# A two-layer decoder trunk on one core: the up projection in seven products of halves as well, in an order that interleaves two pairs

## The chip, the core and the metric

One core of a Trainium2 chip runs the whole program. The metric is the device time of one execution in microseconds (us), as the median over runs; a profile of one further execution gives the trace. TensorE multiplies (a weight load, then a matmul that streams columns), VectorE (DVE) and ScalarE (ACT) do the elementwise work, GpSimd (POOL) a little, and SyncE (SP) issues the DMAs.

## The reference, cut to what matters

The input is 512 tokens of 1024 features in float32. There are two layers; each is a feed-forward block (FFN), a mixer, and another FFN, so four FFNs in all:

```
def swiglu(h, w_gate, w_up, w_down):
    return (jax.nn.silu(h @ w_gate) * (h @ w_up)) @ w_down
...
h = rmsnorm(x, ffn1_norm[i])
x = x + FFN_HALF * swiglu(h, ffn1_w_gate[i], ffn1_w_up[i], ffn1_w_down[i])
```

The inner width is 2816, which is 22 tiles of 128 columns. The mixer of layer 0 pools over windows of tokens; that of layer 1 is latent attention with 8 heads. The change touches only the FFNs, and through one pool of buffers the rest.

## The kernel before

**Layout and precision.** Activations lie with features in partitions: eight tiles of 128 features by 512 tokens. Every float32 operand is cut into a high and a low part (`split`, L114 to L118: ScalarE copies the high part, VectorE subtracts to get the low one), and a product of two operands is three matmuls, high by high, high by low, low by high (`mm3`). So a product of one weight tile (1024 features by 128 columns) with all tokens is 8 x 3 = 24 matmuls of 512 columns. All of them are issued at L106.

**An FFN.** The 22 tiles of gate and up go in thirds: tiles 0 to 7, 8 to 15, 16 to 21. After each third its part of the down projection runs (eight output tiles, L479 adds them to x). Tiles 0 to 3 use x unscaled. From tile 4 on the operand is the normed x (`xn`), and the gate's tiles are taken two at a time by Winograd's form of Strassen's product: `class Two` with seven products of halves in place of eight. A half is 512 features by 256 tokens or by 128 columns of weights, so one such product (`block`) is 4 x 3 = 12 matmuls of 256 columns, and a pair takes 7 x 12 = 84 of them.

**What a pair costs besides.** `w_sums` loads the two weight tiles (L340, L341), makes four sums of their quarters on VectorE (L350, 512 columns each), and splits a11 with a12, s1 with s2, s3 with s4 (1024 columns each) and a22 (512). The products go into two accumulators, each a whole bank, both halves of which are used. Their partial sums are combined by one copy on ScalarE (L379) and five additions of 256 columns on VectorE (L395); silu is L287, the product with up L291.

**Order.** In the thirds from tile 8 on, a pair of tiles is written as: the up product of tile f (`product`, weights by `load_w` with its DMA at L129), the first four blocks of the gate's pair (`begin`), the up product of tile f + 1, the last three blocks (`end`), then silu, multiplication and split. In the first third the four up products of tiles 4 to 7 come first, with the sums of xn (`x_sums`) between them, then the two gate pairs.

**Buffers.** Weights: `raw` 3 buffers, `whi` and `wlo` 3 each; `chi`, `clo` 2 each and `s` 2 for the sums; a22's halves 1 each. `work` has 7, PSUM accumulators 6. The order of instructions on each engine is made by a list scheduler of the framework from the order in the text, and semaphores keep it; each engine then takes its instructions in that order.

Of the kernel before, what the change touches and what calls it, by code (L numbers as in the profile page):

```python
# [18 lines left out]
P = 128  # L19
# [34 lines left out]
def _bits(v, n):  # L54
    """v cut to n significant bits (float64)."""
    m, e = np.frexp(v)
    return float(np.ldexp(np.trunc(np.ldexp(m, n)), e - n))
# [12 lines left out]
def _wrapped(v):  # L70
    """v less the nearest multiple of 2 pi, for an integer v, in extended precision."""
    pi2 = np.longdouble("6.283185307179586476925286766559005768")
    v = np.longdouble(v)
    return float(v - np.rint(v / pi2) * pi2)
# [3 lines left out]
def trunk(ctx: ExitStack, tc: tile.TileContext, a: dict, out: bass.AP):  # L78
# [20 lines left out]
    def work(shape=None):  # L99
        return kp.tile(shape or [P, S], F32, tag="work", name="work", bufs=7)  # L100
# [7 lines left out]
    def mm3(ps, w, x, first, last):  # L108
        """w, x: (hi, lo) pairs; the product's three parts, in one group."""
        mm(ps, w[0], x[0], first, False)  # L110
        mm(ps, w[0], x[1], False, False)
        mm(ps, w[1], x[0], False, last)

    def split(src, hi, lo, scale=None):  # L114
        """hi + lo = src * scale exactly as float32, each with 12 bits."""
# [17 lines left out]
    # ---- x, constants  # L133
# [6 lines left out]
    # the copy's table, ahead of its use  # L140
    nc.scalar.activation(small(1, tag="mx", bufs=6), ones[:, 0:1], AF.Copy)

    # ---- 1/sqrt on [P, n]
# [20 lines left out]
    # ---- x_j: its gained halves for the next layer, and its share of the sum of squares  # L164
    class Prep:
# [23 lines left out]
        def rstd(self):  # L189
            """[P, NT]: token t of tile i in partition t, column i."""  # L190
# [7 lines left out]
        def rstd_rows(self, r):  # L198
            """[P, S]: the same in every partition, tokens along the free axis."""
# [9 lines left out]
    def opening(wg, wu, prep):  # L209
        """the first tile of gate and up, as x and the weights come in."""  # L210
# [47 lines left out]
    def ffn_in(fp, wg, wu, wd, prep, nxt, first, final):  # L258
# [5 lines left out]
        def product(w, x, turned=False, then=None):  # L264
            """then, if given, comes before the last steps"""
# [17 lines left out]
        def gated(zg, zu):  # L283
            """silu(zg) * zu in halves; zg in parts, the last in the tile that is written."""
            z = zg[-1][1]
            for cs, g in zg:
                nc.scalar.activation(z[:, cs], g[:, cs] if g is z else g, AF.Silu)  # L287
            return halved(z, zu)
# [7 lines left out]
        # The first tiles take x unscaled, and their products are scaled by the tokens' 1/rms.  # L296
        # The others take xn, x scaled first, and most of them the gate's tiles two at a time,
        # by seven products of halves (Winograd's form of Strassen's): xn in blocks of 512
        # features by 256 tokens, the weights in blocks of 512 features by 128 columns.
        # Tokens of one size keep these sums as good as float32's own.  # L300
# [5 lines left out]
        def normed(k):  # L306
            """tiles k and KH + k of xn in halves; both stay in float32 as well."""
# [13 lines left out]
        def x_sums(k):  # L321
            """the four sums of xn's blocks, a (hi, lo) pair for each tile of 128 features."""
            b11, b12, b21, b22 = (kept[k][:, c * C : (c + 1) * C] for c in range(4))
# [11 lines left out]
        def w_sums(top, low):  # L335
            """the blocks of two weight tiles, and their four sums, as (hi, lo) pairs."""
# [27 lines left out]
        class Two:  # L364
            """two tiles of columns by seven products, in two steps"""

            def __init__(self, w, f):
                self.w, self.f = w, f

            def begin(self):  # L370
                a11, self.a12, self.a22, s1, s2, s3, self.s4 = w_sums(self.w[self.f], self.w[self.f + 1])
                p, q = self.p, self.q = acc(), acc()
                block(p[:, :C], a11, half(0, 0), True, True)
                block(p[:, C:], s2, summed(1), False, True)
                block(q[:, C:], s3, summed(2), True, True)
                block(q[:, :C], s1, summed(0), False, True)
                self.za, self.zb, u = work(), work(), work()
                self.u = u
                nc.scalar.activation(u[:, :C], p[:, :C], AF.Copy)  # L379
                plus(u[:, :C], p[:, C:], u[:, :C])  # L380
                plus(u[:, C:], q[:, C:], u[:, :C])
                plus(self.zb[:, C:], q[:, :C], u[:, C:])

            def end(self):
                """for each tile the parts it lies in; all but the first are in one tile"""
                p, q, u, za, zb = self.p, self.q, self.u, self.za, self.zb
                block(p[:, :C], self.a12, half(1, 0), False, True)
                block(q[:, C:], self.a22, summed(3), False, True)
                block(q[:, :C], self.s4, half(1, 1), False, True)
                plus(zb[:, :C], q[:, C:], u[:, :C])  # L390
                plus(za[:, C:], q[:, :C], u[:, :C])
                return [(lower, p[:, lower]), (upper, za)], [(slice(0, S), zb)]
# [19 lines left out]
        for f0, f1 in THIRDS:  # L412
            hs = []
            for f in range(f0, f1, 2):
                if f < 4:
                    if first and f == 0:
                        pg, pu = opening(wg[0], wu[0], prep)
                    else:
                        pg = product(wg[f], xh)
                        if f == 2:  # L420
                            normed(0)
                        pu = product(wu[f], xh)
                        if f == 2:
                            normed(1)
                    if rows is None:
                        r = prep.rstd()
                    qg = product(wg[f + 1], xh)
                    if rows is None:
                        rows = prep.rstd_rows(r)
                    zs = scaled(pg), scaled(pu)  # L430
                    if f == 2:
                        normed(2)
                    hs.append(gated([(slice(0, S), zs[0])], zs[1]))
                    qu = product(wu[f + 1], xh)
                    zs = scaled(qg), scaled(qu)
                    if f == 2:
                        normed(3)
                    hs.append(gated([(slice(0, S), zs[0])], zs[1]))
                    continue
                if f == 4:  # L440
                    gates = Two(wg, f), Two(wg, f + 2)

                    def begin():
                        x_sums(3)
                        gates[0].begin()

                    us = []
                    for e in range(f, f + 4):
                        us.append(product(wu[e], xn, e == f, begin if e == f + 3 else None))
                        if e < f + 3:  # L450
                            x_sums(e - f)
                    for e, gate in enumerate(gates):
                        if e:
                            gate.begin()
                        for z, u in zip(gate.end(), us[2 * e :]):
                            hs.append(gated(z, u))
                    continue
                if f == 6:
                    continue
                gate = Two(wg, f)  # L460
                pu = product(wu[f], xn)
                gate.begin()
                qu = product(wu[f + 1], xn)
                za, zb = gate.end()
                hs.append(gated(za, pu))
                hs.append(gated(zb, qu))
            nf = f1 - f0
            for m in range(KD):
                hi, lo = load_w(wd[m][:, f0 * P : f1 * P], nf * P)
                # the last tile of all leaves in two parts  # L470
# [17 lines left out]
    def pool_layer(prep, nxt):  # L488
        """x += scale * (window mean - token) @ w, tokens pooled by a banded product."""
        with tc.tile_pool(name="pp", bufs=1) as pp:  # L490
# [37 lines left out]
            def pools(q, m):  # L528
# [3 lines left out]
                for i in range(NT):  # L532
                    # 256 columns at a time: the band's own, then or before it zeros
# [36 lines left out]
    # ---- rotary tables [P, NT, 64], tokens in partitions; gains taken in  # L570
# [82 lines left out]
    def mla_layer(prep, nxt):  # L653
        with tc.tile_pool(name="mp", bufs=1) as mp:
# [21 lines left out]
            def latent(m):  # L676
                """features in partitions, gained but not yet scaled by their rms."""
# [20 lines left out]
            # shared rotary key  # L698
# [7 lines left out]
            # high parts give the first 64 rows, low parts the others  # L706
# [17 lines left out]
            def rotated(dst, src, tab, heads):  # L724
                """src, dst: [P, NT, heads, 64] views, may be the same."""
# [27 lines left out]
            def latent_rms(e, n):  # L753
                """r / rms of a latent, and its square."""
# [15 lines left out]
            # the exponential's table, ahead of its use  # L770
# [10 lines left out]
            # Generators that yield the matmuls they issued, in columns of 512, so that  # L781
            # one head's attention can be cut into another pair's projections.
            def rsqrt_of(ss, f2, more=None):
                """1 / rms over a head, from sums of squares [P, NT, 2] and their scale."""
# [10 lines left out]
            def project(c, got):  # L795
                """heads 2c, 2c + 1: q, k, v with tokens in partitions; q unscaled, k and v scaled."""
# [357 lines left out]
```

## Time and profile before

| | |
|---|---|
| median of three runs | 1698.85 us (1698.4 to 1699.43) |
| span of the profiled execution | 1697.1 us |
| median less span | 1.75 us |
| TensorE busy | 1683.8 us (99%) |
| VectorE busy | 1076.1 us (63%) |
| ScalarE busy | 702.3 us (41%) |
| granted TensorE clock, mean | 0.999 of full speed |

The profiled execution has only a span of its own; 1.75 us is what the runs show around it. Busy times of TensorE overlap from one matmul to the next, so a matmul's cost is read from the distance between starts, not from its duration. The share of an engine is an average over stages that differ.

### The profile page before, as it was taken

Reading aid. Unit: us, or ns where it says so; the run is one execution under the profiler, and the core shown is the slowest. Engines: PE = TensorE matmul, PEld = TensorE weight load, DVE = VectorE, ACT = ScalarE, POOL = GpSimd, SP = SyncE. Lnnn points to the kernel's source line nnn. Section 1 sums busy time; section 2 is a strip of 40 time slices with the busy share of each in tenths; the row PEclk is TensorE's granted clock in tenths of the full one; section 3 lists DMA queues with packets and bytes.
Section 4 is the critical chain, followed back from the end, with each engine's and each line's share of the span. In section 5 each row is a group of like instructions: output and inputs, shape, how many; then the busy total and the mean of one; then the engine's idle time right before and its main releaser. Section 6 shows DMA issues by size and latency. Waiting matters only on the chain.

```text
span 1697.1 us, 23211 instructions
## 1 busy us (share of the span) xinstructions
PE 1683.8 (99%) x9238; PEld 1462.2 (86%) x9238; DVE 1076.1 (63%) x1824; ACT 702.3 (41%) x1163; POOL 70.1 (4%) x147
## 2 busy tenths in 40 slices
PE   8999999999999999999999999999999999999999
PEld 7888988887888988888889889888888789898897
DVE  8845645698845545569556455646778796465463
ACT  6423423364423423444324223546665453243241
POOL 0000000012000000000000000003321300000000
PEclk9999999999999999999999999999999999999999
DMA  5333332232322332332323323321112123233232
GB/s 176 97 109 97 104 98 97 87 114 76 111 92 95 106 98 96 90 109 88 112 98 102 99 99 89 103 90 52 44 57 88 63 87 106 93 100 106 94 94 93
DMA packets 48204, 161.54 MB, mean 95 GB/s; under 512 B 5728, under 2 KB 6496, under 8 KB 48096
## 3 DMA queue, kind: packets, MB, share of 16 engines
q1 hardware_dynamic: 47520, 159.34, 29.3%
q8 instruction: 72, 1.18, 0.3%
q10 hardware_dynamic: 576, 0.72, 0.1%
q14 instruction: 36, 0.29, 0.1%
HBM read 157.94 MB, written 2.10 MB: 94 GB/s over the span
## 4 chain that ended last, share of the span: by engine, by line
PE 97%; DVE 1%; ACT 0%; issue 0%; DMA 0%; POOL 0%; ACTq 0%; DVEq 0%; POOLq 0%
PE acc L106 95%; PE aux L670 1%; PE aux L106 1%; DVE slot L121 1%; PE aux L951 1%; DVE x L986 0%; DVE wlo L118 0%; DMA gains<-in_gains 0%; DMA pos_i<-in_pos 0%; ACT work L932 0%; DVE x L544 0%; POOL work L937 0%; ACT slot L117 0%; ACT slot L120 0%; ACT whi L117 0%
## 5 line engine op out<-in xcount | busy, mean ns | idle before, releaser
L106 PE MATMUL acc<-slot,whi 128*128 128x512 f32 x3212 | 994.1, 391 | 8.7 <-ACT whi L117 5.2
L106 PEld LDWEIGHTS acc<-slot,whi 128*128 128x128 f32 x3212 | 598.0, 189 | 132.3 <-DVE slot L121 5.5
L106 PE MATMUL acc<-slot,wlo 128*128 128x512 f32 x1598 | 622.2, 390 | 0.0
L117 ACT ACTIVATE whi<-raw 128x1024 fp32r<-128x1024 f32 (+2 forms) x237 | 239.5, 1013 | 526.6 <-PE acc L106 469.2
L118 DVE TENSOR_TENSOR wlo<-raw,whi 128x1024 fp32r<-128x1024 f32 (+2 forms) x236 | 276.4, 1173 | 152.8 <-ACT whi L117 150.9
L106 PEld LDWEIGHTS acc<-slot,wlo 128*128 128x128 f32 x1598 | 300.9, 188 | 63.3 <-DVE wlo L118 1.3
L106 PE MATMUL acc<-slot,hi 128*128 128x256 f32 x1296 | 239.4, 281 | 0.0
L106 PEld LDWEIGHTS acc<-slot,hi 128*128 128x128 f32 x1296 | 204.6, 190 | 5.9
L106 PE MATMUL acc<-slot,lo 128*128 128x256 f32 x648 | 182.4, 281 | 0.0
L479 DVE SCALAR_TENSOR_TENSOR x<-acc,x 128x512 f32<-128x512 f32 (+1 forms) x97 | 66.4, 684 | 169.3 <-PE acc L106 169.3
L117 ACT ACTIVATE hi<-s 128x1024 fp32r<-128x1024 f32 x72 | 76.0, 1060 | 154.7 <-DVE s L350 103.1
L106 PE MATMUL acc<-t,hi 128*128 128x256 f32 x720 | 136.4, 282 | 0.0
L106 PEld LDWEIGHTS acc<-slot,lo 128*128 128x128 f32 x648 | 122.9, 190 | 0.0
L395 DVE TENSOR_TENSOR work<-acc,work 128x256 f32<-128x256 f32 x180 | 72.7, 420 | 64.8 <-ACT work L379 33.1
L106 PEld LDWEIGHTS acc<-t,hi 128*128 128x128 f32 x720 | 110.8, 189 | 0.0
L118 DVE TENSOR_TENSOR lo<-s,hi 128x1024 fp32r<-128x1024 f32 x72 | 87.8, 1224 | 34.3 <-ACT hi L117 33.7
L106 PE MATMUL acc<-t,lo 128*128 128x256 f32 x360 | 101.7, 282 | 0.0
L350 DVE TENSOR_TENSOR s<-raw 128x512 f32<-128x512 f32 x72 | 49.2, 687 | 71.1 <-DMA raw<-in_ffn_gate 71.1
L106 PE MATMUL acc<-whi,slot 128*128 128x384 f32 (+2 forms) x320 | 87.7, 344 | 0.0
L117 ACT ACTIVATE slot<-work 128x512 fp32r<-128x512 f32 x104 | 62.1, 626 | 57.2 <-DVE work L291 50.1
L118 DVE TENSOR_TENSOR slot<-work,slot 128x512 fp32r<-128x512 f32 x104 | 68.8, 687 | 25.1 <-ACT slot L117 25.0
L287 ACT ACTIVATE work<-work 128x512 f32<-128x512 f32 x88 | 43.9, 537 | 59.7 <-DVE work L395 56.6
(184 smaller groups left out, 1478.4 us busy)
## 6 DMA issues: line engine op xcount, KB each, us to landing
raw<-in_ffn_gate SPq DMA_DIRECT2D x87, 512.0 KB, 3.4
raw<-in_ffn_up SPq DMA_DIRECT2D x87, 512.0 KB, 3.4
raw<-in_ffn_down SPq DMA_DIRECT2D x64, 512.0 KB, 3.5
raw<-in_ffn_down SPq DMA_DIRECT2D x32, 384.0 KB, 3.1
raw<-in_w_q SPq DMA_DIRECT2D x12, 384.0 KB, 3.0
raw<-in_w_in SPq DMA_DIRECT2D x8, 512.0 KB, 3.4
raw<-in_w_out SPq DMA_DIRECT2D x8, 512.0 KB, 3.4
x<-in_xT SPq DMA_DIRECT2D x8, 256.0 KB, 5.2
```

Of the source, the lines that this page charges most:

```text
L106: nc.tensor.matmul(ps, lhsT, rhs, start=start, stop=stop, skip_group_check=skip)
L117: nc.scalar.activation(hi, src, AF.Copy)
L118: nc.vector.tensor_tensor(out=lo, in0=src, in1=hi.bitcast(F32), op=ALU.subtract)
L121: nc.vector.scalar_tensor_tensor(out=lo, in0=src, scalar=scale, in1=hi.bitcast(F32), op0=ALU.mult, op1=ALU.subtract)
L287: nc.scalar.activation(z[:, cs], g[:, cs] if g is z else g, AF.Silu)
L350: nc.vector.tensor_tensor(out=out, in0=x, in1=y, op=op)
L395: nc.vector.tensor_tensor(out=out, in0=x, in1=y, op=ALU.add)
L479: nc.vector.scalar_tensor_tensor(out=xs[m][:, cs], in0=p[:, cs], scalar=0.5, in1=xs[m][:, cs], op0=ALU.mult, op1=ALU.add,)
L670: nc.tensor.transpose(p[:, i * P : (i + 1) * P], src(i), ident)
L951: nc.tensor.transpose(p[:, js], self.pr[i][:, js], ident)
```

## The change

From tile 8 on, the up projection's tiles too are taken in pairs by seven products of halves. `Two` is written anew: `r` (one half of a bank) collects products 1, 6, 5, 3 in turn and `q` (a whole bank) collects 7 and 4 in its upper half and 2 in its lower one. ScalarE copies the partial sums after products 1, 6 and 7 into `kept`; VectorE adds after product 5 (256 columns) and after product 4 (512 columns). Pairs are interleaved by `twos`: while one pair does its last three products, the next does its first four. `x_sums` takes the token halves in exchanged roles. `work` has 6 buffers in place of 7, tiles `z` (3) and `m` (2) are new, and the scratch for DMA descriptors is set to 1024. In the first third, two of the four up products are copied to SBUF by ScalarE, and the two gate pairs go through `twos`. The rest of the diff deletes comments.

```
-        return kp.tile(shape or [P, S], F32, tag="work", name="work", bufs=7)
+        return kp.tile(shape or [P, S], F32, tag="work", name="work", bufs=6)
...
-            b11, b12, b21, b22 = (kept[k][:, c * C : (c + 1) * C] for c in range(4))
+            b12, b11, b22, b21 = (kept[k][:, c * C : (c + 1) * C] for c in range(4))
...
-            def begin(self):
-                a11, self.a12, self.a22, s1, s2, s3, self.s4 = w_sums(self.w[self.f], self.w[self.f + 1])
...
+            def load(self):
+                a11, a12, a22, s1, s2, s3, s4 = w_sums(*self.w)
+                self.r, self.q = acc()[:, :C], acc()
+                self.z = fp.tile([P, 2 * S], F32, tag="z", name="z", bufs=3)
+                self.kept = fp.tile([P, 3 * C], F32, tag="m", name="m", bufs=2)
+                r, q = self.r, self.q
+                ql, qu = q[:, :C], q[:, C:]
+
+                self.products = {
+                    1: (r, a11, half(0, 1), True, False), 6: (r, s2, summed(1), False, False),
+                    5: (r, s1, summed(0), False, False), 3: (r, s4, half(1, 0), False, True),
+                    7: (qu, s3, summed(2), True, False), 2: (ql, a12, half(1, 1), False, False),
+                    4: (qu, a22, summed(3), False, True),
+                }
+
+            def product(self, n):
+                block(*self.products[n])
+                c = [slice(e * C, (e + 1) * C) for e in range(4)]
+                if n in (1, 6, 7):
+                    part = self.r if n != 7 else self.q[:, C:]
+                    nc.scalar.activation(self.kept[:, c[(1, 6, 7).index(n)]], part, AF.Copy)
+                elif n == 5:
+                    plus(self.z[:, c[2]], self.r, self.kept[:, c[2]])
+                elif n == 4:
+                    z = self.z.rearrange("p (e b t) -> p e b t", e=2, b=2)[:, :, 1]
+                    two = "p (e t) -> p e t"
+                    plus(
+                        z, self.q.rearrange(two, e=2), self.kept[:, : 2 * C].rearrange(two, e=2)
+                    )
+
+        def twos(todo):
+
+            last = None
+            for two in (*todo, None):
+                if two:
+                    two.load()
+                if not last or not two:
+                    one = last or two
+                    for n in (5, 4, 3) if last else (1, 7, 6, 2):
+                        one.product(n)
+                else:
+                    for one, n in (
+                        (last, 5), (two, 1), (last, 4), (two, 7), (two, 6), (last, 3), (two, 2)
+                    ):
+                        one.product(n)
+                if last:
+                    yield last
+                last = two
+
+        def silu(two):
+            nc.scalar.activation(two.z[:, :C], two.r, AF.Silu)
+            nc.scalar.activation(two.z[:, C:], two.z[:, C:], AF.Silu)
+            return two.z
+
+        def times(z, two):
+            for cs, u in ((slice(0, C), two.r), (slice(C, 2 * S), two.z[:, C:])):
+                nc.vector.tensor_mul(z[:, cs], z[:, cs], u)
+            for e in range(2):
+                h = slot(), slot()
+                split(z[:, e * S : (e + 1) * S], *h)
+                hs.append(h)
...
+            if f0 == 0:
+                us, zu = [], None
+                for e in range(4, 8):
+                    u = product(wu[e], xn, e == 4)
+                    if e < 6:
+                        zu = zu if zu is not None else fp.tile([P, 2 * S], F32, tag="z", name="z", bufs=3)
+                        z = zu[:, (e - 4) * S : (e - 3) * S]
+                        nc.scalar.activation(z, u, AF.Copy)
+                        u = z
+                    us.append(u)
+                    x_sums(e - 4)
+                for e, gate in enumerate(twos([Two(wg, 4), Two(wg, 6)])):
+                    z = silu(gate)
+                    for i, u in enumerate(us[2 * e : 2 * e + 2]):
+                        hs.append(halved(z[:, i * S : (i + 1) * S], u))
+            else:
+                z = None
+                for e, two in enumerate(twos([Two(w, f) for f in range(f0, f1, 2) for w in (wg, wu)])):
+                    if e % 2 == 0:
+                        z = silu(two)
                     else:
-                        pg = product(wg[f], xh)
...
-                gate = Two(wg, f)
-                pu = product(wu[f], xn)
-                gate.begin()
-                qu = product(wu[f + 1], xn)
-                za, zb = gate.end()
-                hs.append(gated(za, pu))
-                hs.append(gated(zb, qu))
+                        times(z, two)
```

## Rows read from the trace of the kernel before

**Rows 1.** The page: engines over the span, clock by slices, the chain.
```profile
PE 1683.8 (99%) x9238; PEld 1462.2 (86%) x9238; DVE 1076.1 (63%) x1824; ACT 702.3 (41%) x1163; POOL 70.1 (4%) x147
PEclk9999999999999999999999999999999999999999
PE acc L106 95%; PE aux L670 1%; PE aux L106 1%; DVE slot L121 1%; PE aux L951 1%; DVE x L986 0%; DVE wlo L118 0%; DMA gains<-in_gains 0%; DMA pos_i<-in_pos 0%; ACT work L932 0%; DVE x L544 0%; POOL work L937 0%; ACT slot L117 0%; ACT slot L120 0%; ACT whi L117 0%
```

**Rows 2.** Waits of TensorE, whole span (total us, times, longest).
```profile
PE acc L106 <- ACT whi L117: 5.2, 1, 5.2
PE acc L106 <- DVE slot L121: 3.3, 2, 2.8
```

**Rows 3.** Windows of one pair (blocks, product, blocks, product): length, then busy PE, PEld, DVE, ACT, POOL.
```profile
144.62:150.34 5.72, 5.72 (x49) 5.72 (x48) 1.65 (x2) 1.45 (x2) 0.00 (x0) 1.00 0.31 95
150.34:155.83 5.49, 5.49 (x26) 4.51 (x25) 4.29 (x7) 2.04 (x2) 0.00 (x0) 1.00 0.20 57
155.83:160.09 4.26, 4.26 (x38) 4.25 (x36) 4.01 (x4) 3.04 (x5) 0.00 (x0) 1.00 0.31 102
160.09:165.57 5.48, 5.48 (x27) 4.51 (x26) 3.51 (x7) 2.13 (x5) 0.00 (x0) 1.00 0.46 153
sum 20.95, PE 20.95 PEld 18.99 DVE 13.46 ACT 8.66 POOL 0.00; mean PE 5.24 PEld 4.75 DVE 3.37 ACT 2.17 POOL 0.00
```

**Rows 4.** Windows: two gate pairs in a row, a third's last pair, an FFN's start.
```profile
72.88:85.63 12.75, 12.75 (x98) 12.24 (x96) 10.88 (x15) 5.42 (x7) 0.00 (x0) 1.00 0.42 125
85.63:95.62 9.99, 9.99 (x86) 9.99 (x85) 7.14 (x12) 4.75 (x8) 0.00 (x0) 1.00 0.39 120
313.82:335.34 21.52, 21.30 (x134) 18.76 (x132) 10.05 (x21) 6.35 (x11) 0.00 (x0) 1.00 0.29 80
...
1350.00:1404.00 54.00, 54.00 (x247) 44.66 (x246) 46.41 (x86) 27.55 (x38) 0.00 (x0) 1.00 0.26 88
```

**Rows 5.** VectorE by line and shape, 95.62 to 330 us: count, busy, mean ns.
```profile
L118 DVE TENSOR_TENSOR lo<-s,hi 128x1024 fp32r<-128x1024 f32 x14 | 17.2, 1225 | 8.0 <-ACT hi L117 7.9
L395 DVE TENSOR_TENSOR work<-acc,work 128x256 f32<-128x256 f32 x37 | 14.9, 420 | 14.9 <-ACT work L379 8.3 <-PE acc L106 6.4
...
L350 DVE TENSOR_TENSOR s<-raw 128x512 f32<-128x512 f32 x14 | 9.6, 688 | 17.9 <-DMA raw<-in_ffn_gate 17.9
```

**Rows 6.** ScalarE by line and shape, 95.62 to 330 us: count, busy, mean ns.
```profile
L117 ACT ACTIVATE hi<-s 128x1024 fp32r<-128x1024 f32 x14 | 14.8, 1060 | 34.1 <-DVE s L350 23.8 <-PE acc L106 10.3
...
L287 ACT ACTIVATE work<-work 128x512 f32<-128x512 f32 x8 | 5.1, 632 | 13.7 <-DVE work L395 13.7
...
L379 ACT ACTIVATE work<-acc 128x256 f32<-128x256 f32 x7 | 2.7, 385 | 14.2 <-PE acc L106 14.2
L287 ACT ACTIVATE work<-acc 128x256 f32<-128x256 f32 x7 | 2.5, 364 | 0.0
```

**Rows 7.** Timeline of VectorE, 301 to 309 us: start, duration.
```profile
301.59 0.68 DVE L350 TENSOR_TENSOR s<-raw 128x512 f32<-128x512 f32 x1
302.19 0.68 DVE L350 TENSOR_TENSOR s<-raw,s 128x512 f32<-128x512 f32 x1
...
306.69 1.23 DVE L118 TENSOR_TENSOR lo<-s,hi 128x1024 fp32r<-128x1024 f32 x1 [0.27 <-ACT hi L117]
307.83 0.69 DVE L118 TENSOR_TENSOR lo<-raw,hi 128x512 fp32r<-128x512 f32 x1
```

**Rows 8.** Timelines of TensorE and ScalarE about the end of a bank's second block.
```profile
75.74 0.40 PE L106 MATMUL acc<-t,hi 128*128 128x256 f32 x2
...
76.00 0.39 ACT L379 ACTIVATE work<-acc 128x256 f32<-128x256 f32 x1 [3.83 <-PE acc L106]
```

**Rows 9.** DMA issues (queue, count, KB each, us to landing), and a wait on them.
```profile
raw<-in_ffn_up SPq DMA_DIRECT2D x87, 512.0 KB, 3.4
...
DVE s L350 <- DMA raw<-in_ffn_gate: 71.1, 32, 3.6
```

More of the change, by code (lines that the diff above doesn't have):

```diff
@@ L367, in __init__ @@
             def __init__(self, w, f):
-                self.w, self.f = w, f
-            def begin(self):
-                a11, self.a12, self.a22, s1, s2, s3, self.s4 = w_sums(self.w[self.f], self.w[self.f + 1])
[L372 to L392, printed above, removed]
+                self.w = w[f], w[f + 1]
@@ L413, in ffn_in @@
             hs = []
[L414 to L417, printed above, removed]
-                    else:
-                        pg = product(wg[f], xh)
[L420 to L453, printed above, removed]
-                            gate.begin()
[L455 to L459, printed above, removed]
-                gate = Two(wg, f)
-                pu = product(wu[f], xn)
-                gate.begin()
-                qu = product(wu[f + 1], xn)
-                za, zb = gate.end()
-                hs.append(gated(za, pu))
-                hs.append(gated(zb, qu))
@@ new lines, in ffn_in @@
+            for f in range(f0, min(f1, 4), 2):
+                if first and f == 0:
+                    pg, pu = opening(wg[0], wu[0], prep)
+                else:
+                    pg = product(wg[f], xh)
+                    if f == 2:
+                        normed(0)
+                    pu = product(wu[f], xh)
+                    if f == 2:
+                        normed(1)
+                if rows is None:
+                    r = prep.rstd()
+                qg = product(wg[f + 1], xh)
+                if rows is None:
+                    rows = prep.rstd_rows(r)
+                zs = scaled(pg), scaled(pu)
+                if f == 2:
+                    normed(2)
+                hs.append(gated([(slice(0, S), zs[0])], zs[1]))
+                qu = product(wu[f + 1], xh)
+                zs = scaled(qg), scaled(qu)
+                if f == 2:
+                    normed(3)
+                hs.append(gated([(slice(0, S), zs[0])], zs[1]))
@@ new lines, in ffn_in @@
+            if f0 == 0:
[13 more added lines that the diff above has]
+                        hs.append(halved(z[:, i * S : (i + 1) * S], u))
+            else:
+                z = None
+                for e, two in enumerate(twos([Two(w, f) for f in range(f0, f1, 2) for w in (wg, wu)])):
+                    if e % 2 == 0:
+                        z = silu(two)
+                    else:
+                        times(z, two)
@@ L1141 @@
     arrays |= _constants()
-    nc = bacc.Bacc("TRN2", target_bir_lowering=False, num_devices=1)
+    nc = bacc.Bacc(
+        "TRN2", target_bir_lowering=False, num_devices=1, dynamic_dma_scratch_size=1024
+    )
     aps = {
```

## The prediction

> **What bounds the kernel now.** The page comes first. TensorE is busy for 99% of the span, its granted clock stands in the highest tenth in every slice, which is the 2.4 GHz level, and 95% of the chain that ended last lies on the matmuls of L106 [rows 1]. So time changes when matmuls go away, or when something makes TensorE wait. The waits of TensorE say how rare the second is: the two largest kinds come to 8.5 us in the whole span, three waits in all [rows 2]. VectorE at 63% and ScalarE at 41% are averages [rows 1]; the windows give them for the stage that changes. A pair of tiles from tile 8 on takes 20.95 us, in which TensorE never stops, VectorE works 13.46 us and ScalarE 8.66 us [rows 3].
>
> **What the change takes away.** The same windows price both kinds of product [rows 3]. Seven blocks (84 matmuls of 256 columns) take 5.72 + 4.26 = 9.98 us, or 0.119 us a matmul. Two whole products (48 matmuls of 512 columns) take 5.49 + 5.48 = 10.97 us, or 0.2285 us a matmul. A narrow matmul costs 0.52 of a wide one and there are 1.75 as many, so seven blocks in place of two products save 10.97 - 9.98 = 0.99 us. Tiles 8 to 21 are seven pairs; four FFNs make 28 pairs, and 28 x 0.99 = 27.7 us. The first third keeps its matmuls, and down projection, pooling and attention are not touched.
>
> The weight load limits the narrow matmul: in the first window of blocks the loads are busy for all 5.72 us, in the whole products only 4.51 of 5.49 [rows 3]. The Trainium skill, TensorE: Matmul & The Clock Gate, section Back-to-back issue gap, gives N / 2.4 + 2.5 ns for an isolated matmul of N columns. By that, as an estimate, 48 x 215.8 less 84 x 109.2 ns is 1.19 us a pair, 33 us in all. The trace is dearer at both widths (228.5 and 119 ns), so the measured distances decide.
>
> **What it adds on VectorE.** I count per pair of gate and up. Each `Two` makes four sums of 512 columns at 0.69 us, three splits of 1024 at 1.23, one of 512 at 0.69, and now one addition of 256 at 0.42 and one of 512 at 0.69 [rows 5]: 2.76 + 3.69 + 0.69 + 1.11 = 8.25 us. Two make 16.5. `times` adds a product of 256 columns (0.42), one of 768 (between the rows of 512 and 1024, 0.96) and two splits of 512 (1.38), 2.76 in all. That makes 19.3 us. The same count for before is 14.4 us: one set of sums and splits 7.14, five additions 2.1, two weight splits 2.46, two products and two splits of 512 2.76. The window has 13.46 us busy in place of 14.4, because the next instruction starts before the last one's end: the sum at 301.59 lasts 0.68 and the next starts after 0.60; the split at 306.69 lasts 1.23 and the next starts after 1.14 [rows 7]. In that proportion 19.3 becomes 18.0 us, in 2 x 9.98 = 19.96 us of TensorE: 90%. The Trainium skill speaks against relying on that overlap: VectorE: DVE Perf Modes, section The DRAIN you can't avoid, says that the next operation does not start until the pipe is empty, and allows an earlier start only where nothing holds it. If every one were held, the load would be the full 19.3 us, 97%, still below TensorE's time. The trace shows starts 0.08 us before ends, so I take 90%.
>
> **What it adds on ScalarE.** Each `Two` splits three times 1024 at 1.06 and once 512 at 0.63, and copies three times 256 at 0.385 [rows 6]: 4.97 us. Two of them, silu of 256 and 768 columns (0.36 and about 0.85) and two high parts of 512 (1.26) are 12.4 us of 19.96, 62%. It has room.
>
> **Whether the interleaved order covers the handovers.** Time 0 is the start of product 5 of the earlier pair L; a block is 1.43 us; the order is L5, N1, L4, N7, N6, L3, N2. Signals from TensorE to ScalarE take about 0.26 us: the last block of a bank ends at 75.74 and the copy starts at 76.00 [rows 8].
> - N's s1 and s2 need the weight buffer that L's a12 held until 0: 0.26 + 1.06 + 1.23 + 0.2 for the signal is 2.75; N6 asks at 5.71. Margin 3.0.
> - N's s3 and s4 need the buffer of L's predecessor, free at -1.43, and are asked at 4.28. Margin 3.0 with nothing in front.
> - The copy of N1 has from 2.86 to 5.71; the addition after L5 from 1.43 to 7.14; the copy of N7 from 5.71 to 8.57, because N2 writes the other half of the bank; the copy of N6 from 7.14 to 10.0. Each needs 0.7 to 0.9 us.
> - VectorE's batch after L3 (8.57) is the largest: `times` 2.76, s3/s4 of the next pair 1.23, s1/s2 1.23, sums 2.76. Back to back it ends near 16.6, and the addition after N5, queued behind, near 17.0; N3 asks for it at 17.1. This is the thinnest margin, about 0.
> - DMA brings 1 MB per 9.98 us, as before 2 MB per 20.95. A load lands in 3.4 us, and the sums waited up to 3.6 us for one [rows 9]; a buffer freed near 6.4 and refilled by about 10 is asked at about 13.
>
> So in the steady part I take 0 for waits, with 0.3 us a `Two` as the upper bound (the signal's own length). Two places show such loads without a stop: in 85.63 to 95.62 seven blocks follow seven others directly in 9.99 us, with VectorE at 10.88 of 12.75 us just before, and from 1350 to 1404 TensorE works all 54.00 us beside a VectorE busy for 46.41, 86% [rows 4].
>
> **Where the cover is gone.** Four FFNs with three thirds make 12 chains of pairs. At the end (5, 4, 3 without another pair) the addition after 5 has 1.43 us; it takes 0.7, but behind a split of 1.23 on VectorE it takes 1.95, so TensorE waits 0 to 0.5. At the start (1, 7, 6, 2) three copies have 1.43 us each; each takes 0.65, or 1.7 behind a split of 1.06 on ScalarE: 0 to 0.3 each. That is 0 to 1.4 us a chain; the free case is nearer, as the down projection loads both engines lightly, so I take 0.4, 12 x 0.4 = 4.8 us. A third's last pair before took 21.52 us, 0.57 more than 20.95 [rows 3, 4]; this wait may go (four times 0.57, 2.3 us), which I leave in the lower bound. One `work` buffer fewer costs 0: the additions of 256 columns that used them have left, and attention and squares are not near six at a time by the program's order; the upper bound is a second wait like the largest of TensorE, 5.2 us [rows 2].
>
> **Sum.** Against the profiled execution: 1697.1 - 27.7 + 4.8 = 1674.2 us of span, and the 1.75 us around it, 1676.0 us. The median of the runs shown is 1698.85.
>
> **The rivals.**
> - *VectorE becomes the bound in part.* Its instructions go in order, so idle moments cannot all be used. For it speaks 90% busy and the margin of 0 above; against it the windows with 85 to 86% beside a full TensorE [rows 4]. At 0.1 to 0.4 us a `Two`, 56 x 0.1 to 0.4 is 6 to 22 us more, 1682 to 1698.
> - *The saving is eaten exactly.* At about 0.5 us a `Two` the 27.7 us are gone: 1699. It is the end of the first rival.
> - *Slower: the handover of the weight buffer.* s1/s2 of the pair that follows an up pair is split only after product 2 has freed its buffer. If the list puts `times`, s3/s4 and the sums ahead of it (2.76 + 1.23 + 2.76 = 6.75 us), the chain of 2.75 becomes 9.5 against 5.71: TensorE waits 3.8 us. That occurs after an up pair inside a chain, 3 + 2 times an FFN, 20 times: 76 us, less 27.7 - 4.8, gives 1752. It decides from 27.7 / 20 = 1.4 us a time on. Against it: the gate pairs in a row before took 9.99 us without such a wait [rows 4].
> - *More gain.* No wait at the ends and the third's last wait gone: 1676.0 - 4.8 - 2.3 = 1669.
>
> **How the numbers follow.** Within 0.2% (3.4 us) is about what a measurement of this kernel cannot tell from no change. The forecast, 1669 to 1682, has 0.66; still less 0.03; VectorE in part, 1682 to 1695, 0.15; the saving eaten, 1695 to 1702, 0.06; slower 0.10. The predicted time is the likeliest case's, 1676. A range of 1669 to 1692 leaves out the 0.03 below and about 0.17 above. Faster 0.84, the same 0.06, slower 0.10.
>
> **What would show it.** Right: 1344 fewer matmuls of 512 columns and 2352 more of 256, at 0.119 us from start to start; a gate and up pair in 20.0 us with VectorE busy for about 18 of them; waits of TensorE in the thirds only at the chains' ends. Wrong: waits of the weight loads on L118 or on the additions inside chains, which would be the rivals, or a distance between narrow matmuls over 0.13 us, which alone would take the saving.

## The result, and the profile after

The changed kernel takes 1674.55 us (median of four runs) against 1699.14 for the one before in the same runs. The ratio is 0.9853, with a 95% interval of 0.9839 to 0.9867: 24.6 us less. The forecast was 1676.0 us, with a range of 1669 to 1692. Two single executions, one of experiment e2 and one of a1, ran hundreds of us longer at a lower mean clock (0.75 and 0.66), and the medians given here leave them out.

The page of the changed kernel, its first part and part of the groups (after the bar: busy us, mean ns of one, idle before). They answer to [rows 1]:

```profile
span 1672.8 us, 25532 instructions
PE 1659.1 (99%) x10246; PEld 1491.9 (89%) x10246; DVE 1182.8 (71%) x1940; ACT 800.7 (48%) x1347; POOL 69.7 (4%) x147
...
L106 PE MATMUL acc<-slot,hi 128*128 128x256 f32 x2304 | 424.6, 281 | 0.1
L106 PE MATMUL acc<-slot,lo 128*128 128x256 f32 x1152 | 324.3, 282 | 0.0
```

TensorE is still busy for 99% of a span that is 24.3 us shorter (1697.1 less 1672.8). It has 1008 matmuls more, which is 2352 narrow ones less 1344 wide ones. VectorE rose by 106.7 us of work and still did not become the bound.

Windows of the first chain of eight pairs of tiles (tiles 8 to 15, gate and up) in the changed kernel: length, then busy PE, PEld, DVE, ACT, POOL. They answer to [rows 3]:

```profile
139.51:159.51 20.00, 20.00 (x169) 20.00 (x168) 12.69 (x18) 10.69 (x16) 0.00 (x0) 1.00 0.25 79
159.51:179.51 20.00, 20.00 (x170) 20.00 (x169) 17.84 (x26) 11.76 (x18) 0.00 (x0) 1.00 0.34 107
179.51:199.51 20.00, 20.00 (x171) 20.00 (x170) 17.47 (x25) 11.76 (x18) 0.00 (x0) 1.00 0.34 106
199.51:219.50 19.99, 19.99 (x171) 19.99 (x170) 13.83 (x19) 10.42 (x16) 0.00 (x0) 1.00 0.39 114
sum 79.99, PE 79.99 PEld 79.99 DVE 61.83 ACT 44.63 POOL 0.00; mean PE 20.00 PEld 20.00 DVE 15.46 ACT 11.16 POOL 0.00
```

A gate and up pair takes 20.0 us for its 168 narrow matmuls, 0.119 us each, where [rows 3] had 20.95: 0.95 us less. TensorE never stops in the chain. VectorE works 17.5 to 17.8 us in the two middle windows, but only 12.7 and 13.8 in the first and the last, since the first pair's sums are made ahead of the chain.

The waits of the weight loads in the changed kernel (total us, times, longest), the four largest kinds that wait for an engine's result; the fourth is new:

```profile
PEld acc L106 <- ACT whi L117: 6.0, 4, 5.1
PEld acc L106 <- DVE slot L121: 4.8, 4, 3.2
...
PEld acc L106 <- DVE wlo L118: 2.2, 6, 0.6
PEld acc L106 <- DVE z L434: 1.9, 4, 0.5
```

The new kind is the addition after product 5 (`plus`, L434 there), four times, once an FFN. The timelines of TensorE and VectorE show it at the end of the chain in the first FFN's first third (start, duration):

```profile
94.73 0.39 PE L106 MATMUL acc<-slot,wlo 128*128 128x512 f32 x1
95.16 0.50 PE L106 MATMUL acc<-slot,hi 128*128 128x256 f32 x2
...
92.94 1.23 DVE L118 TENSOR_TENSOR wlo<-raw,whi 128x1024 fp32r<-128x1024 f32 x1 [0.26 <-ACT whi L117]
94.08 0.69 DVE L118 TENSOR_TENSOR slot<-z,slot 128x512 fp32r<-128x512 f32 x1
94.68 1.02 DVE L434 TENSOR_TENSOR z<-acc,m 128x256 f32<-128x256 f32 x2
```

VectorE splits a weight tile and part of the first pair's result before it comes to the addition at 94.68; product 3 starts at 95.16. The list even put three wide matmuls of the down projection into the gap: the third starts at 94.73, and the next matmul follows after 0.43 us in place of 0.23. So TensorE itself loses 0.2 us here, less than the 0.5 for which the weight load waits.

To see where the 24.3 us came from, I measured each trace by stages, from the start of the last addition onto x in one stage to that of the next (L479 before, L511 after):

```
us            before    after     less
first thirds  FFN 1-3   139.36 125.93 131.01   140.02 126.54 131.63   -1.89
second thirds FFN 1-4   127.31 x4              123.62, 123.52 x3      15.06
last thirds   FFN 1-4   96.11 95.57 95.71 95.80   93.14 92.32 92.33 92.55   12.85
pooling                 26.89                  26.54                   0.35
attention and FFN 4's first third  378.40      380.45                 -2.05
sum                                                                   24.32
```

The second thirds give 3.76 us each for four pairs, which is about four times 0.95. By these marks the first thirds lose 0.6 each, and the last thirds give 3.21 for three pairs, 0.36 more than three times 0.95. But the marks are VectorE's, and one of them moved. TensorE and VectorE at the end of the first FFN's first third, before:

```profile
139.16 0.62 PE L106 MATMUL acc<-slot,whi 128*128 128x512 f32 x2
139.36 0.69 DVE L479 SCALAR_TENSOR_TENSOR x<-acc,x 128x512 f32<-128x512 f32 x1 [2.44 <-PE acc L106]
```

And in the changed kernel, where the addition stands behind a split:

```profile
139.51 0.40 PE L106 MATMUL acc<-slot,hi 128*128 128x256 f32 x2
138.88 1.23 DVE L118 TENSOR_TENSOR lo<-s,hi 128x1024 fp32r<-128x1024 f32 x1 [1.13 <-ACT hi L117]
140.02 0.68 DVE L511 SCALAR_TENSOR_TENSOR x<-acc,x 128x512 f32<-128x512 f32 x1
```

TensorE starts the next third 0.20 us ahead of the mark before (139.16 to 139.36) and 0.51 ahead of it after (139.51 to 140.02). At an FFN's last mark (FFN 2 and 3) it is 0.20 in both. So 0.31 us of each first third's loss is time that the last third shows as gain. By TensorE's own starts a first third loses 0.3 us, of which 0.2 is the wait above, and the last thirds of FFN 2 to 4 give 2.9 to 3.1, about 0.1 more than three times 0.95. Of the 2.05 us in the last row 0.6 is such a mark and such a loss, and 1.4 us remain.

These 1.4 us go with TensorE's clock. Windows of 20 us about the end of the attention stage, the first of the changed kernel, the second of experiment e6 below (the column behind POOL is the mean granted clock):

```profile
1313.00:1333.00 20.00, 17.21 (x66) 13.69 (x65) 14.12 (x14) 9.08 (x14) 10.09 (x6) 0.83 0.20 65
```
```profile
1310.00:1330.00 20.00, 16.43 (x72) 12.96 (x70) 16.48 (x16) 11.10 (x18) 11.71 (x7) 1.00 0.20 55
```

A mean of 0.83 over 20 us is 6.8 us at 1.2 GHz, the rest at 2.4. In the kernel before the same stretch had a mean of 0.91, so 3.6 us. TensorE stands still for 2.8 us in the first window shown and for 3.6 in the second, so the length of the waits alone doesn't decide whether the clock falls. The four runs of the changed kernel show what the low stretch is worth: three have a mean clock of 0.998 and spans of 1672.7 to 1672.8 us, the fourth has 1.000 and 1670.2 us.

### The profile page after: what moved, and what is told of

Same layout as the page of the kernel before. It is cut to its first block, busy times and chain, and to the rows that moved or that the text cites. A ratio compares the mean times of both kernels' runs of the same rounds, so it can differ in the third digit from the quotient of the medians.

```text
span 1672.8 us, 25532 instructions
## 1 busy us (share of the span) xinstructions
PE 1659.1 (99%) x10246; PEld 1491.9 (89%) x10246; DVE 1182.8 (71%) x1940; ACT 800.7 (48%) x1347; POOL 69.7 (4%) x147
## 4 chain that ended last, share of the span: by engine, by line
PE 97%; DVE 2%; ACT 1%; issue 0%; DMA 0%; POOL 0%; ACTq 0%; DVEq 0%; POOLq 0%
PE acc L106 95%; PE aux L702 1%; PE aux L106 1%; DVE slot L121 1%; PE aux L983 0%; DVE x L1018 0%; DVE wlo L118 0%; ACT work L964 0%; DMA gains<-in_gains 0%; DVE x L576 0%; ACT slot L117 0%; ACT slot L120 0%; ACT whi L117 0%; POOL work L969 0%; ACT work L852 0%
## 5 line engine op out<-in xcount | busy, mean ns | idle before, releaser
L106 PE MATMUL acc<-slot,whi 128*128 128x512 f32 x2428 | 752.4, 391 | 8.4 <-ACT whi L117 5.1
L106 PEld LDWEIGHTS acc<-slot,whi 128*128 128x128 f32 x2428 | 454.9, 189 | 102.8 <-ACT whi L117 5.6
L106 PE MATMUL acc<-slot,wlo 128*128 128x512 f32 (+1 forms) x1206 | 470.6, 390 | 0.0
L106 PE MATMUL acc<-slot,hi 128*128 128x256 f32 x2304 | 424.6, 281 | 0.1
L106 PEld LDWEIGHTS acc<-slot,hi 128*128 128x128 f32 x2304 | 356.9, 189 | 2.9 <-DVE z L434 1.9
L117 ACT ACTIVATE whi<-raw 128x1024 fp32r<-128x1024 f32 (+2 forms) x181 | 179.8, 996 | 333.8 <-PE acc L106 261.4
L106 PE MATMUL acc<-slot,lo 128*128 128x256 f32 x1152 | 324.3, 282 | 0.0
L106 PE MATMUL acc<-t,hi 128*128 128x256 f32 x1280 | 242.9, 282 | 0.0
L117 ACT ACTIVATE hi<-s 128x1024 fp32r<-128x1024 f32 x128 | 135.1, 1058 | 139.9 <-PE acc L106 89.4
L511 DVE SCALAR_TENSOR_TENSOR x<-acc,x 128x512 f32<-128x512 f32 (+1 forms) x97 | 66.3, 684 | 136.9 <-PE acc L106 136.9
L117 ACT ACTIVATE hi<-raw 128x512 fp32r<-128x512 f32 (+1 forms) x128 | 107.9, 843 | 83.6 <-PE acc L106 65.6
L118 DVE TENSOR_TENSOR lo<-raw,hi 128x512 fp32r<-128x512 f32 (+1 forms) x128 | 121.0, 953 | 0.0
L106 PEld LDWEIGHTS acc<-t,lo 128*128 128x128 f32 x640 | 120.5, 188 | 0.0
```

The lines of the kernel that those rows point to most:

```text
L106: nc.tensor.matmul(ps, lhsT, rhs, start=start, stop=stop, skip_group_check=skip)
L117: nc.scalar.activation(hi, src, AF.Copy)
L118: nc.vector.tensor_tensor(out=lo, in0=src, in1=hi.bitcast(F32), op=ALU.subtract)
L511: nc.vector.scalar_tensor_tensor(out=xs[m][:, cs], in0=p[:, cs], scalar=0.5, in1=xs[m][:, cs], op0=ALU.mult, op1=ALU.add,)
```

## The experiments

All are edits of the changed kernel, except e5, which edits the one before. Ratios are against the kernel before, on the same chip.

**e1: up by whole products again.**

```
-                for e, two in enumerate(twos([Two(w, f) for f in range(f0, f1, 2) for w in (wg, wu)])):
...
+                for f in range(f0, f1, 2):
+                    two = Two(wg, f)
+                    us = [product(wu[f], xn)]
+                    two.load()
+                    for n in (1, 7, 6, 2):
+                        two.product(n)
+                    us.append(product(wu[f + 1], xn))
+                    for n in (5, 4, 3):
+                        two.product(n)
...
```

> From tile 8 on the up projection goes back to whole products; the new accumulators, buffers and gate pairs stay. Theory (the saving is the seven products): a gate and up pair costs 0.95 to 0.99 us more again, 28 x 0.95 to 0.99 = 27 to 28 us, so about 1701 us, with VectorE busy for about 13 of 21 us of a pair. Rival (the saving came from the new accumulators or buffers): it stays below 1685 us.

Measured: 1702.18 us, ratio 1.0021 (1.0012 to 1.0031). The window of a pair in e1:

```profile
144.62:165.57 20.95, 20.95 (x133) 19.02 (x132) 12.59 (x16) 9.37 (x13) 0.00 (x0) 1.00 0.30 101
```

The pair is back at 20.95 us, and the kernel at 27.6 us over the changed one. 28 x 0.95 is 26.6. So the whole saving is the seven products; the new accumulators and buffers save nothing by themselves (this kernel takes 3.3 us more than the one before). VectorE has less to do than in [rows 3], 12.59 us against 13.46, and it changes nothing.

**e2: no interleaving.**

```
...
-                        (last, 5), (two, 1), (last, 4), (two, 7), (two, 6), (last, 3), (two, 2)
...
+            for two in todo:
+                two.load()
+                for n in (1, 7, 6, 2, 5, 4, 3):
+                    two.product(n)
+                yield two
```

> Every pair does its seven products in one go, 1, 7, 6, 2, 5, 4, 3, before the next pair begins. Theory (the interleaving is what covers the copies and additions; without it each has one block of 1.43 us): at the 0.4 us a pair of tiles taken for an uncovered handover, 64 x 0.4 = 26 us more, about 1700 us. Rival (the engines have room enough and the list of instructions fills the gaps): below 1680 us.

Measured: 1691.36 us, ratio 0.9955 (0.9939 to 0.9972), so 16.8 us more than the changed kernel. That is between the two expectations. The waits of the weight loads in e2:

```profile
PEld acc L106 <- DVE z L423: 15.7, 31, 1.2
```

It is the addition after product 5 again, which here has one block of TensorE, 1.43 us, as cover. It is late at 31 of the 56 pairs of tiles in the second and last thirds, by 0.5 us on average, and at none of the eight in the first thirds. In the trace each of the 31 stands right behind a split of 1024 columns on VectorE. The second and last thirds are 19.2 us longer than in the changed kernel by the stage lengths, and these waits are 15.7 of them; what the rest is was not shown. The other stages are 2.4 us shorter, 1.5 of it in the stretch with attention, where this run had the full clock. Without the interleaving about two thirds of the saving would be lost.

**e3 and e4: more work for VectorE.** The sum s4 is made twice or three times; the result is the same. The line added in e4:

```
                 (s3, a11, a21, ALU.subtract), (s4, a12, s2, ALU.subtract),
+                (s4, a12, s2, ALU.subtract), (s4, a12, s2, ALU.subtract),
```

> The sum s4 of each pair of weight tiles is made twice: 0.6 us more VectorE work for each of 64 pairs of tiles, 38 us in all; a gate and up pair then has about 19.2 of 20.0 us on VectorE. Theory (VectorE has 10% room and is not the bound): at most 5 us more, 1680 us. Rival (VectorE is already the bound in part): 15 to 38 us more, 1690 to 1712 us.

> The sum s4 is made three times: 1.2 us more VectorE work for each of 64 pairs of tiles, so 10.2 us of VectorE for 9.99 us of TensorE. Theory (room of 1.0 us a pair of tiles): VectorE becomes the bound by 0.2 us a pair at least, and with waits that don't fit more, 10 to 40 us more, 1685 to 1715 us. Rival (in-order waits leave no room at all): 77 us more, 1750 us.

Measured: 1677.78 us (0.9879, 0.9864 to 0.9894) and 1678.28 us (0.9881, 0.9866 to 0.9896). The time of e3 is as expected, but its 3.2 us do not lie in the chains of eight, which take 123.6 to 123.8 us in three of four FFNs as against 123.5. They lie in the first thirds, where a copy of ScalarE comes late:

```profile
PEld acc L106 <- ACT m L392: 3.7, 4, 1.0
```

e4 has no such wait. It is a miss: 77 us of additional work cost 3.7 us (by the stage lengths 4.7 outside the stretch with attention, where its profile had the full clock). By the stage lengths its chains of eight got 0.5 to 0.7 us longer. So "room of 1.0 us a pair of tiles", taken from the middle of a chain, was too small.

**e8 and e10: more still.** The same edit with s4 made four and six times.

> The sum s4 is made four times: 1.8 us more VectorE work for each pair of tiles. With 17.5 us busy per gate and up pair in the changed kernel (its trace), that is 21.1 us for 19.99 us of TensorE. Theory (VectorE is the next bound and reaches TensorE's time at about 1.2 us more): the steady part of the chains now goes at VectorE's pace, 0.55 us a pair of tiles more, about 50 of them, 20 to 40 us more than the changed kernel, 1695 to 1715 us. Rival (buffers and semaphores, not VectorE's time, set the pace): again only 3 to 5 us more, below 1682 us.

> The sum s4 is made six times: 3.0 us more VectorE work for each pair of tiles. In the changed kernel a chain of eight pairs of tiles has 80.0 us of TensorE and 61.8 us of VectorE within it (windows of its first chain), since the first pair's sums are made ahead and the last pair's products fall behind. Theory (what counts is the whole chain: room of 18.2 us, 2.3 us a pair of tiles): eight times 3.0 is 24 us, of which some 2 to 3 fall outside, so a chain gets 3 to 6 us longer, a chain of six somewhat less, the gates of the first third some 3 us: 44 us in four FFNs, 1705 to 1740 us. Rival (the steady pair of the chain's middle, 17.5 of 20 us, sets the pace: (8.75 + 3.0 - 10.0) x 50): 88 us more, 1755 to 1770 us. Second rival (VectorE's load isn't what counts): below 1695 us.

Measured: 1682.86 us (0.9906, 0.989 to 0.9923) and 1752.03 us (1.0323, 1.0304 to 1.0342). e8 too is a miss: it lies 12 us under the range of the theory and 0.9 over the rival's bound. The first chain of eight as one window, in e4, e8 and e10:

```profile
139.04:219.72 80.68, 80.35 (x673) 80.07 (x672) 69.64 (x96) 45.15 (x69) 0.00 (x0) 1.00 0.33 101
```
```profile
139.70:221.01 81.31, 81.03 (x673) 80.35 (x672) 73.28 (x103) 45.11 (x69) 0.00 (x0) 1.00 0.32 98
```
```profile
140.85:234.25 93.40, 86.06 (x681) 83.45 (x680) 84.54 (x120) 45.95 (x69) 0.00 (x0) 0.98 0.28 91
```

The chain is a batch with a start and an end, not a steady state. VectorE's share of it goes from 61.8 of 80.0 us to 69.6, 73.3 and 84.5; as long as the sum stays below TensorE's 80 us, the chain grows by 0.7 and 1.3 us only. In the middle of e8's chain VectorE hardly stops, and TensorE does not stop at all; what VectorE has still to do falls into the last window, which is 1.3 us longer:

```profile
159.70:179.70 20.00, 20.00 (x170) 19.98 (x169) 19.90 (x30) 11.53 (x18) 0.00 (x0) 1.00 0.35 102
179.70:199.70 20.00, 20.00 (x168) 19.81 (x167) 19.90 (x30) 11.11 (x18) 0.00 (x0) 1.00 0.28 85
```

In e10, with 84.5, the window grows by 13.4 us. It holds eight matmuls of the down projection (x681), 1.8 us, and the clock stood at 1.2 GHz for 3 to 4 us of it (0.98 on the mean); by the stage lengths the second third grows by 11.6. In the middle of e10's chain VectorE is nearly never idle, and TensorE is:

```profile
180.85:200.85 20.00, 16.98 (x139) 16.37 (x138) 19.76 (x29) 10.27 (x16) 0.00 (x0) 1.00 0.27 84
```

The largest kind of wait of the weight loads in e10 is for ScalarE's copies of high parts, some of which wait for VectorE's sums in turn (`ACT hi L117 <- DVE s L351`, 4.8 us from 160 to 215):

```profile
PEld acc L106 <- ACT hi L117: 41.1, 24, 2.9
```

Both ranges given for e10 missed: 1752 lies 12 us over the chain's rule and 3 under the steady one. The excess of VectorE over 80 us was estimated rightly (4.5 us; 3 to 6 were given), but the chain grew by two and a half to three times that, because VectorE is idle for 8.9 us of the window all the same. That the sums wait for buffers there, and the last pair's work for the last products, is argued from the order of the program, not shown. So the total over the chain tells whether the work fits; once it does not, the steady rule came nearer. VectorE becomes the bound somewhere between 1.8 and 3.0 us of its work more for each pair of tiles.

**e5: the `work` buffer alone.**

```
-        return kp.tile(shape or [P, S], F32, tag="work", name="work", bufs=7)
+        return kp.tile(shape or [P, S], F32, tag="work", name="work", bufs=6)
```

> The kernel before with 6 work buffers in place of 7 and nothing else. Theory (the buffer costs nothing): 1699 us, within 1.5 us; the attention stage, about 210 us, as long as before. Rival (the buffer is why the stretch from the second layer's first FFN to its second got 1.4 us longer): 1.4 us more, in that stage alone.

Measured: 1699.49 us, ratio 1.0002 (0.9993 to 1.0011). The stretch of attention and the next first third is 378.63 us against 378.40. In the kernel before, the buffer costs nothing that can be measured.

**e6: the wait at the end of the first third.**

```
-                for e, gate in enumerate(twos([Two(wg, 4), Two(wg, 6)])):
+                for e, gate in enumerate(list(twos([Two(wg, 4), Two(wg, 6)]))):
```

> In the first third of each FFN, silu, multiplication and split of the first gate pair are written after the last products of the second pair. Theory (the addition after product 5 waits behind that work on VectorE at the chain's end): the four waits of TensorE on this addition, 1.9 us in all, go, and each first third gets about 0.5 us shorter; 2 us in all, about 1672.5 us where the clock does not differ. Rival (the addition waits for its semaphore anyway): the waits stay.

Measured: 1672.0 us, ratio 0.9843 (0.9829 to 0.9856). The waits on the addition fell, they did not go:

```profile
PEld acc L106 <- DVE z L434: 0.9, 4, 0.2
```

By the stage lengths the first thirds of FFN 1 to 3 became 0.50, 0.13 and 0.15 us shorter, less than the 0.5 expected of each. The larger part of the 2.5 us against the changed kernel is the stretch with attention, 378.66 against 380.45 us, where this run had the full clock throughout (the second window above). That the time is so near the 1672.5 expected is luck. The clock alone brings most of it: the changed kernel's own runs at a mean clock of 1.000 have spans of 1670.2 us (result) and of 1671.2 and 1671.8 (a1), the four of e6 have 1670.0 to 1670.9. At the same clock the edit gains about 1 us at most.

**e7 and e9: a third pair in the first third's chain.** Up tiles 6 and 7 also go by seven products; in e9 the subtractions of `x_sums` are moved to GpSimd as well.

```
-                for e in range(4, 8):
-                    u = product(wu[e], xn, e == 4)
...
+                for e in range(4, 6):
+                    us.append(product(wu[e], xn, e == 4))
+                    x_sums(2 * e - 8)
+                    x_sums(2 * e - 7)
+                z = None
+                for e, two in enumerate(twos([Two(wg, 4), Two(wg, 6), Two(wu, 6)])):
...
```

> Up tiles 6 and 7 go by seven products too, so the first third has three pairs in its chain and two whole products ahead of it. Theory (what counts is matmul time as long as VectorE keeps up): 4 x 0.95 = 3.8 us less, about 1671 us, if the sums of xn and of the weights are ready in time. Rival (the two products were the cover of the sums of xn): they take 11 us of cover away per FFN while the sums of xn, some 12 us of VectorE, and of the first weights stay; TensorE waits 3 to 10 us an FFN and the time rises to 1685 to 1710 us.

> As the kernel with three pairs in the first third, but the 16 subtractions of the sums of xn go to GpSimd. Theory (there VectorE, busy without a gap from 54 to 71 us, was what TensorE waited for): 16 x 0.42 = 6.7 us an FFN leave VectorE, the waits of 4.5 us an FFN go, and the third pair's 4 x 0.95 us are won: 1668 to 1676 us. Rival (GpSimd is slower: 1.6 us for 512 columns in the attention stage, so about 0.85 us for 256, 14 us in a chain): the sums are late still, 1680 to 1692 us.

Measured: 1694.42 us (0.9976, 0.9967 to 0.9985) and 1692.16 us (0.9962, 0.9947 to 0.9976), both some 18 to 20 us slower than the changed kernel. The rivals were right (e9 lies just over the 1692 that its rival gave). The weight loads of e7 wait four times, once an FFN, for low parts that VectorE splits off for the first pair:

```profile
PEld acc L106 <- DVE lo L118: 19.0, 4, 4.7
```

Windows of 10 us at the start of the first third's chain, of e7 and of e9:

```profile
66.00:76.00 10.00, 6.42 (x42) 6.42 (x43) 9.34 (x12) 4.46 (x7) 0.00 (x0) 0.83 0.34 105
```
```profile
66.00:76.00 10.00, 7.67 (x51) 7.67 (x52) 8.33 (x11) 4.83 (x8) 0.00 (x0) 0.83 0.38 126
```

TensorE stands still for 3.6 and 2.3 us there, while VectorE is busy with the sums and splits, and the clock falls on top: a mean of 0.83 is 3.4 us at 1.2 GHz. So the two whole products that e7 takes away had covered that work, as the rival says. GpSimd does not help enough. Most of its subtractions of 256 columns take 1.06 to 1.20 us where 0.85 was expected, and it waits for `work` buffers; its timeline in e9:

```profile
55.03 1.12 POOL L327 TENSOR_TENSOR work<-chi 128x256 f32<-128x256 f32 x1 [0.80 <-DVE work L291]
56.22 1.07 POOL L327 TENSOR_TENSOR work<-chi,work 128x256 f32<-128x256 f32 x1
```

**a1: the changed kernel again.**

> The changed kernel once more, beside the others of this call. Expected 1672 to 1674.6 us: its four runs were 1672.04 and three of 1674.5, and the granted clock of the profiled one shows a stretch of 6.8 us at 1.2 GHz at the end of the attention stage. If that stretch makes the two values, a profile without it has a span of about 1670.5 us.

Measured: 1673.59 us (median of three runs, 1673.0 to 1675.5 us); ratio 0.9855 (0.9838 to 0.9871). Its profile has a span of 1673.7 us, a mean clock of 0.998 and again 0.83 in the window from 1313 to 1333 us. The two other runs have a mean clock of 1.000 and spans of 1671.2 and 1671.8 us. So here, as in the four runs of the result, the low stretch goes with 1.9 to 2.6 us. No profile of this kernel without the low stretch was had, so where those us lie within the run is not shown.

No version tried beats the changed kernel beyond the intervals.

## Why the prediction was right

- **The saving.** 0.99 us a pair was forecast from the windows, 0.95 measured (20.95 less 20.00), so 26.6 us in place of 27.7. The narrow matmul was right at 0.119 us; the four blocks and three blocks of [rows 3] added up to 9.98 and the chain shows 10.0. e1 shows that nothing else in the change saves time.
- **VectorE.** 18.0 us a pair was forecast, 17.5 to 17.8 measured in a chain's middle. That the next instruction starts before the last one's end is seen again: in the timeline above the split at 92.94 lasts 1.23 us and the next starts after 1.14. The rule of the Trainium skill (VectorE: DVE Perf Modes, The DRAIN you can't avoid), which taken for every instruction would have given 19.3 us, is too dear for this stream; the load measured agrees with the exception it makes.
- **The handovers.** Taken at 0 within the chains, and the trace shows no wait of TensorE or of its weight loads inside a chain of the second and last thirds. The signals were taken too long: the 0.26 us to ScalarE run from 75.74, which is the start of the next block, while the last matmul of the block is recorded from 75.62 to 75.90, 0.10 before the copy. No run shows the 0.2 us for the signal behind the split. Both only make the margins of 3.0 us larger. The reasoning was too careful in one more place: the "thinnest margin, about 0" of the addition behind VectorE's batch was worked out as if the middle of a chain went on for ever. e4 put 1.2 us more into each pair of tiles and the chains of eight grew by 0.5 to 0.7 us. The chain's total decides whether the work fits, as e4 and e8 show; e10 shows that it does not tell the price once it doesn't.
- **Where the cover is gone.** 12 ends at 0.4 us, 4.8 us, were forecast. Measured are four waits of weight loads of 0.5, 1.9 us, and only in the first third, where VectorE still has the first pair's result to finish; the eight other ends wait for nothing. By TensorE's starts a first third loses 0.3 us, 1.2 in all. The mechanism is the one named, a short addition behind a long split, and e2 shows it at 31 places, each behind a split of 1024 columns, once the cover is taken away.
- **Left in the lower bound.** The wait after the last thirds (0.57 us was read from [rows 4]) gave little: about 0.1 us in FFN 2 to 4. The stage table's 3.21 in place of 2.85 is for the most part the mark that moved.
- **Not foreseen.** 1.4 us went with a longer stretch at 1.2 GHz at the end of attention. The sum fits to 1.4 us because three sizes were off in different directions: 1.1 us too much saving, 3.6 us too much waiting at ends, and the clock not counted. That they cancel so far is luck; the saving alone, right to 4%, is not.
- **The rivals.** The slower one, the weight buffer handed over late behind VectorE's batch, did not occur. VectorE as the bound occurs only in e10, so from somewhere between 1.8 and 3.0 us more work a pair of tiles.

## What to carry to other kernels

Where TensorE never waits, price a rewrite of its products by the distance between starts at each width in a window of the trace, here 0.119 and 0.2285 us; seven halves for eight then pay 9%, not 12.5%. Here products with copies and additions between them kept the whole of that saving only with other products in between (a third of it was left in e2), and the end of such a chain is the place to look for what is lost. For a helper engine, add up its work over the whole chain from start to end to see whether it fits, and don't take the middle of a short chain for a steady state; once the total does not fit, the middle's pace is the better guide to the price.

## What the runs showed of the hardware that was not expected

The granted clock fell to 1.2 GHz for 3.4 to 6.8 us just behind the attention stage in some profiles (before and changed, TensorE idle for 2.8 us of 20) and not in others (e6, idle for 3.6); what decides it stays open. In e9 GpSimd took 1.06 to 1.20 us for most of its float32 subtractions of 256 columns, beside a VectorE that was nearly always busy; VectorE takes 0.42.
